# Moving gathered products past the additions into Y: a quota per operation instead of a common limit

## The chip, the core and the metric

The kernel runs on one core of one Trainium2 chip. The metric is device microseconds of one execution, from the first to the last instruction and what lies around them; the time of a kernel is the median of three runs. The engines are TensorE (PE in the rows; PEld is its weight load), VectorE (DVE), ScalarE (ACT), GpSimd (POOL), and SyncE (SP), which issues most transfers. Each engine works through its own instructions in the order in which they were written, and an instruction that waits holds up everything behind it on that engine.

## The reference, cut to what matters

One layer of an encoder: attention and retention, a normalization, and then a feed-forward layer with product keys (PEER), which is where the change lies. For each token `x` the layer picks 8 x 16 = 128 of 16,384 experts, with weights `g`:

```
act = gelu(einsum('tpkd,td->tpk', u_tab[eidx], x))
w   = g * act
out = einsum('tpk,tpkd->td', w, v_tab[eidx])
h   = layer_norm(ALPHA * h + out)
```

There are 1024 prompt tokens and 64 sample tokens, of 1024 channels each.

## The kernel before, in words

The tokens are cut into nine tiles of 128 rows: eight of the prompt and one, `TS`, of the sample. All run through the head first (projections, attention, retention, top-k), up to about 1290 us. Then comes the *dense stage*, the function `dense`, which does the experts in two ways at once.

- **Dense tiles** (five, `DENSE`): all 16,384 experts are computed on TensorE, 128 at a time. For each of the 128 blocks there is a *projection* `u_mm`: 48 matmuls into the PSUM tile `pA`, then a GELU on ScalarE, then on VectorE the product `ge` of it with the routing weights `gt`. Blocks go in groups of three (`BGS`). For each group come ten *value products* `v_mm`, one for each tile `t` and half `h` of the channels: nine matmuls into a PSUM tile `y`, of which there are two buffers (`pY`, `bufs=2`), and then on VectorE the addition of `y` into the SBUF tile `Y`. A third value product can only start when the addition of the first has read its buffer.
- **Gathered tiles** (four: `TS`, 5, 6 and 7): only the chosen experts are computed, on VectorE. A *slot* is one expert of each of the 128 tokens: GpSimd issues an indirect transfer (the *gather*, 128 rows of 8 KB, line 239) into one of four buffers `uv` (`NB = 4`); VectorE multiplies it with the tokens and sums (the *product*, out `uv`); ScalarE does the GELU and the weight (`gav`); VectorE adds the weighted row into `pacc` (the *accumulation*). There are 448 slots. The function `slot` writes one of these two instructions at each call, in turns: product of slot k, then accumulation of slot k-1. So a buffer is read for the last time by the accumulation that stands behind the next slot's product, and the gather four slots later waits for that.

The order on VectorE is decided while the program is written. `dense` is a generator that stops twice in each operation: after the matmuls are written, and after the work behind them is written (`ge`, or the addition into `Y`). At each stop the main loop calls `pump(most)`, which writes up to `2 * most` calls of `slot`, as long as a running estimate of the engines' times (`est`) says that VectorE is not ahead of TensorE and that the gather should have arrived. What is written at the first stop of a `v_mm` stands on VectorE ahead of its addition into `Y`. `prefetch` writes the next gathers, up to three slots ahead (`LEAD = 3`).

When the last slot of a gathered tile is accumulated, `finish` normalizes the tile. It goes on by one step (one `yield`) with each accumulation of the next tile: it loads the two rows of `ln2` into a tile `lnx`, which is one of the four gather buffers, takes statistics, and writes the two scaling instructions in `norm_out`. For `TS` it first moves half of the sum across partitions with a transfer and adds it.

All those instructions are recorded through one helper, so their line in the rows is L108; they are told apart by their tiles.

Of the kernel before, what the change touches and what calls it, by code (L numbers as in the profile page):

```python
# [52 lines left out]
ROOM = -0.3  # L53
# [82 lines left out]
def hymba_peer_step(ctx, tc, a, o):  # L136
# [16 lines left out]
    def rows_bcast(ap, n):  # L153
        return bass.AP(tensor=ap.tensor, offset=ap.offset, ap=[[0, 128], [1, n]])
# [51 lines left out]
    def halves(t):  # L206
        return [t[:, 0:512], t[:, 512:1024]]
# [4 lines left out]
    ctl = dict(most=3, k=0, issued=0, done=-1, avail=[0.0] * len(slots), fin=[], uvp=None, ln2=None, gps=None, lead=LEAD, slack=9.0, cr=0.0, pe0=0.0, dve0=0.0, ph=0, pq=0.0)  # L212
# [19 lines left out]
    def issue():  # L232
        k = ctl["issued"]
        t, j = slots[k]
        if t not in tl:
            open_tile(t)
        R = ctl["uvp"].tile([128, 2 * D], F32, name="uv", tag="uv")
        rows_uv[k] = R
        nc0.gpsimd.indirect_dma_start(out=R, out_offset=None, in_=a["uv"],  # L239
                                      in_offset=bass.IndirectOffsetOnAxis(ap=tl[t]["idx"][:, j:j + 1], axis=0))  # L240
        est.t["pool"] += 1.04
        ctl["pq"] = max(ctl["pq"], now()) + GTC
        est.t["dma"] = max(est.t["dma"], max(est.t["pe"], est.t["dve"]) - 3.0) + 2.6
        ctl["avail"][k] = max(est.t["dma"] + 2.0, max(ctl["pq"], now()) + ctl["slack"])
        ctl["issued"] = k + 1
# [25 lines left out]
    def finish(t, d):  # L271
        r, q = d["acc"], 128
        ln2, late = ctl["ln2"], t == TS
        if ln2 is None or t == TS:
            x = ctl["uvp"].tile([128, 2 * D], F32, name="lnx", tag="uv")
            ln2 = [x[:, 0:D], x[:, D:2 * D]]
            nc.sync.dma_start(ln2[0], rows_bcast(a["ln2_g"], D))
            if t == TS:
                q = NS
                nc.sync.dma_start(ln2[1][0:NS], r[NS:128])  # L280
                yield
                yield
                yield
                yield
                nc.vector.tensor_tensor(r[0:NS], r[0:NS], ln2[1][0:NS], op=OP.add)
            nc.sync.dma_start(ln2[1], rows_bcast(a["ln2_b"], D))
        yield from norm_out(gat, t, r, q, ln2)

    def norm_out(pool, t, r, q, ln2, st=None):
        wide = st is not None  # L290
        if not wide:
            st = pool.tile([128, 2, 6], F32, name="stf", bufs=2)
            for i, x in enumerate(halves(r)):
                nc.vector.bn_stats(st[:q, i], x[:q])
        mv = pool.tile([128, 3], F32, name="mvf", bufs=2)
        nc.vector.bn_aggr(mv[:q, 0:2], st[:q])
        nc.vector.tensor_scalar(mv[:q, 1:2], mv[:q, 1:2], EPS, None, op0=OP.add)
        nc.gpsimd.tensor_tensor(mv[:q, 2:3], mv[:q, 1:2], epsc[:q, 0:1], op=OP.pow)
        if wide:
            nc.gpsimd.tensor_tensor(mv[:q, 0:1], mv[:q, 0:1], mv[:q, 2:3], op=OP.mult)  # L300
            nc.gpsimd.tensor_scalar(mv[:q, 0:1], mv[:q, 0:1], -1.0, None, op0=OP.mult)
            yield
            nc.scalar.activation(r[:q], r[:q], AF.Identity, bias=mv[:q, 0:1], scale=mv[:q, 2:3])
            yield
            nc.gpsimd.tensor_tensor(r[:q], r[:q], ln2[0][:q], op=OP.mult)
            yield
            eng = nc.gpsimd if DENSE.index(t) in PAD else nc.vector
            eng.tensor_tensor(r[:q], r[:q], ln2[1][:q], op=OP.add)
            nc.sync.dma_start(o["y_p"][t * 128:(t + 1) * 128, :], r)
            return  # L310
        for _ in range(4):
            yield
        nc.vector.scalar_tensor_tensor(r[:q], r[:q], mv[:q, 0:1], ln2[0][:q], op0=OP.subtract, op1=OP.mult)
        yield
        nc.vector.scalar_tensor_tensor(r[:q], r[:q], mv[:q, 2:3], ln2[1][:q], op0=OP.mult, op1=OP.add)
        if t == TS:
            nc.sync.dma_start(o["y_s"], r[:q])
        else:
            nc.sync.dma_start(o["y_p"][t * 128:(t + 1) * 128, :], r)

    def can_slot():
        k = ctl["k"]
        return ctl["uvp"] is not None and k < len(slots) and ready[slots[k][0]]

    def prefetch():
        if ctl["uvp"] is None:
            return
        while (ctl["issued"] < len(slots) and ctl["issued"] < ctl["k"] + ctl["lead"]
               and ready[slots[ctl["issued"]][0]]):
            issue()  # L330
# [30 lines left out]
    def now():  # L361
        return max(est.t["pe"], est.t["dve"])
# [29 lines left out]
    def pump(most, room=1.0):  # L392
        prefetch()
        most = 2 * most
        while (can_slot() or ctl["ph"]) and most > 0:
            if est.t["dve"] > est.t["pe"] + room or (not ctl["ph"] and ctl["avail"][ctl["k"]] > now()):
                break
            slot()
            most -= 1
# [14 lines left out]
    bg, kind = [], []  # L414
# [823 lines left out]
    def dense(hx):  # L1238
# [205 lines left out]
        outs = []  # L1444
        for n, (kind, i) in enumerate(ops):
            last = kind == "v" and i[0] == NG - 1
            ctl["most"] = 4
            if n == SL[1]:
                ctl["slack"] = SL[2]
            if 2 <= n < 2 + NT:  # L1450
                nc.sync.dma_start(Y[:, n - 2], spill[DENSE[n - 2]]["h1"])
            if kind == "u":
                if i % 2 == 0:
                    g_load(i // 2 + 1)
                yield from u_mm(i)
            else:
                yield from v_mm(*i)
                if n == len(ops) - 2 * NT - 1:
                    ctl["ln2"] = [vp.tile([128, NT * 256], F32, name="ln2r", tag="gt", bufs=2)[:, 0:D] for _ in range(2)]
                    for x, k in zip(ctl["ln2"], ("ln2_g", "ln2_b")):  # L1460
                        nc.sync.dma_start(x, rows_bcast(a[k], D))
            if last:
                if can_slot():
                    slot()
                for g in outs:
                    next(g, None)
                if i[1]:
                    outs.append(norm_out(xp, DENSE[i[2]], Y[:, i[2]], 128, ctl["ln2"], yst[i[2]]))
            yield
# [14 lines left out]
    with ExitStack() as hx:  # L1484
        for _ in dense(hx):
            for _ in range(NBG):
                if ctl["uvp"] is not None and est.t["dve"] < est.t["pe"] + 1.0:
                    step_bg()
            pump(ctl["most"], ROOM)
        log("dense")  # L1490
        while bg:
            step_bg()
        drain()
# [112 lines left out]
```

## Time and profile before

| what | us |
|---|---|
| median of three runs (3319.77 to 3331.34) | 3320.02 |
| the profiled execution | 3355.53 |
| its span, first to last instruction | 3353.8 |

The profile is of one execution, which took 3355.53 us, some 35 us more than the median of the runs without a profile. Its span falls into the head (to about 1290 us), the part of the dense stage in which gathers run (1290 to 3130 us), the rest of the dense stage (to 3320 us) and an end of 34 us.

### The profile page before, as it was taken

The page shows a single profiled execution, that of the slowest core. Times are in us where ns is not written, and L with a number is a line of the kernel's source. Part 1 is how long each engine was busy: PE and PEld are TensorE (multiplying, and loading weights), DVE is VectorE, ACT ScalarE, POOL GpSimd, SP SyncE. Part 2 cuts the span into 40 slices and gives each one's busy share as a digit, 9 for nine tenths or more (in the row PEclk, how much of TensorE's full clock was granted, in tenths as well). Part 3 has the DMA queues.
Part 4 walks back from the last instruction along what each step waited for, and adds up shares of the span by engine and source line. Part 5 has one row for each costly group of instructions (what it writes and reads, how often), then busy time and mean ns, then how long its engine had stood idle before and what let it go on. Part 6 is the DMA issues. An engine that isn't in the chain of part 4 may idle for free.

```text
span 3353.8 us, 43782 instructions
## 1 busy us (share of the span) xinstructions
PE 2904.7 (87%) x15212; PEld 2495.5 (74%) x15212; DVE 2265.5 (68%) x5539; ACT 1115.8 (33%) x2599; POOL 1781.7 (53%) x1326
## 2 busy tenths in 40 slices
PE   4999889898996568888899988989899899989996
PEld 3777767677775557777788877878788788878895
DVE  1436976738639964776777777777778677877424
ACT  2332232332424663333333333333333333333221
POOL 0000155676663555665666666666666566666544
PEclk8999899899897789999999999999999999999998
DMA  6435235436432468898999989899989899999531
GB/s 178 145 112 213 82 84 145 95 62 167 97 79 79 114 181 325 326 346 304 349 355 354 350 336 340 321 347 341 355 323 361 318 349 349 351 367 340 199 98 63
DMA packets 296470, 813.19 MB, mean 242 GB/s; under 512 B 58296, under 2 KB 164520, under 8 KB 229176
## 3 DMA queue, kind: packets, MB, share of 16 engines
q0 software_dynamic: 97792, 469.94, 39.3%
q1 hardware_dynamic: 198024, 340.12, 29.9%
q8 instruction: 120, 1.97, 0.2%
q14 instruction: 102, 0.84, 0.1%
q10 hardware_dynamic: 432, 0.33, 0.0%
HBM read 753.04 MB, written 56.97 MB: 242 GB/s over the span
## 4 chain that ended last, share of the span: by engine, by line
PE 39%; DVE 22%; DMA 13%; issue 11%; POOL 10%; ACT 3%; SPq 1%; POOLq 0%; DVEq 0%; ACTq 0%
PE pA L108 13%; PE y L108 10%; DMA uv<-uv,gi 9%; PE pv L108 4%; PE pq L108 4%; DVE VI L108 4%; PE pa L108 3%; POOL uv L239 3%; POOL vl L108 3%; DVE pacc L108 3%; DVE ge L108 2%; DVE ob L108 2%; POOL ul L108 2%; POOL wl L108 2%; DVE oh L108 2%
## 5 line engine op out<-in xcount | busy, mean ns | idle before, releaser
L239 POOL DMA_INDIRECT uv<-uv,gi x448 | 432.1, 965 | 619.8 <-DVE pacc L108 561.2
L373 POOL DMA_INDIRECT G<-sg,si x256 | 382.3, 1493 | 620.2 <-DVE si L108 383.3
L108 DVE SCALAR_TENSOR_TENSOR uv<-uv,ph 128x1024 f32<-128x1024 f32 x448 | 544.1, 1215 | 238.1 <-DMA uv<-uv,gi 234.0
L108 PE MATMUL y<-vh,wh 128*128 128x512 f32 x1280 | 530.7, 415 | 185.1 <-DVE Y L108 182.9
L108 DVE SCALAR_TENSOR_TENSOR pacc<-uv,gav,pacc 128x1024 f32<-128x1024 f32 x448 | 575.6, 1285 | 2.2 <-ACT pacc L108 2.1
L108 PE MATMUL y<-vl,wh 128*128 128x512 f32 x1280 | 521.7, 408 | 2.0 <-POOL vl L108 2.0
L108 PE MATMUL y<-vh,wl 128*128 128x512 f32 x1280 | 520.8, 407 | 0.0
L108 PEld LDWEIGHTS y<-vh,wh 128*128 128x128 f32 x1280 | 250.8, 196 | 270.8 <-DVE Y L108 173.6
L108 DVE TENSOR_TENSOR Y<-y,Y 128x512 f32<-128x512 f32 x420 | 280.6, 685 | 178.8 <-PE y L108 175.1
L108 POOL TENSOR_TENSOR vl<-vr,vh 128x512 fp32r<-128x512 f32 x256 | 327.9, 1294 | 100.5 <-ACT vh L108 49.9
L108 PEld LDWEIGHTS pA<-xhi,uh 128*128 128x128 f32 x2048 | 331.5, 199 | 37.1 <-DVE ge L108 24.1
L108 PE MATMUL pA<-xhi,uh 128*128 128x320 f32 x2048 | 338.6, 320 | 23.3 <-DVE ge L108 23.3
L108 ACT ACTIVATE gav<-gav 128x1 f32<-128x1 f32 x448 | 88.7, 198 | 706.5 <-DVE uv L108 693.7
L108 PE MATMUL pA<-xlo,uh 128*128 128x320 f32 x2048 | 321.7, 309 | 0.0
L108 PE MATMUL pA<-xhi,ul 128*128 128x320 f32 x2048 | 321.2, 309 | 0.0
L108 POOL TENSOR_TENSOR ul<-ur,uh 128x1024 fp32r<-128x1024 f32 x128 | 309.6, 2418 | 4.8 <-ACT uh L108 2.5
L108 PEld LDWEIGHTS pA<-xlo,uh 128*128 128x128 f32 x2048 | 306.5, 188 | 0.0
L108 PEld LDWEIGHTS pA<-xhi,ul 128*128 128x128 f32 x2048 | 305.6, 187 | 0.0
L108 PEld LDWEIGHTS y<-vh,wl 128*128 128x128 f32 x1280 | 252.9, 198 | 57.0
L108 PEld LDWEIGHTS y<-vl,wh 128*128 128x128 f32 x1280 | 252.5, 197 | 48.9 <-POOL vl L108 2.9
L108 ACT ACTIVATE pA<-pA 128x640 f32<-128x640 f32 x128 | 88.0, 688 | 511.9 <-PE pA L108 505.9
L108 DVE TENSOR_TENSOR ge<-pA,gt 128x640 f32<-128x640 f32 x128 | 105.2, 822 | 212.0 <-ACT pA L108 145.3
(287 smaller groups left out, 4385.4 us busy)
## 6 DMA issues: line engine op xcount, KB each, us to landing
ur<-ut SPq DMA_DIRECT2D x128, 512.0 KB
vr<-vt SPq DMA_DIRECT2D x256, 256.0 KB
gt<-G SPq DMA_DIRECT2D x320, 128.0 KB
w<-w_r SPq DMA_DIRECT2D x32, 1024.0 KB
G<-gs SPq DMA_DIRECT2D x24, 1024.0 KB
G<-zeros SPq DMA_DIRECT2D x16, 1024.0 KB
w<-w_out SPq DMA_DIRECT2D x16, 1024.0 KB
w<-w_pq SPq DMA_DIRECT2D x16, 1024.0 KB
```

What stands on the lines that cost most here:

```text
L108: return f(*a, **k)
L239: nc0.gpsimd.indirect_dma_start(out=R, out_offset=None, in_=a["uv"], in_offset=bass.IndirectOffsetOnAxis(ap=tl[t]["idx"][:, j:j + 1], axis=0))
L373: nc0.gpsimd.indirect_dma_start(out=spill[t]["G"], out_offset=bass.IndirectOffsetOnAxis(ap=idx[:, j:j + 1], axis=0), in_=g[:, j:j + 1], in ...
```

## The change

The limit at each stop is replaced by a quota. At the first stop of a projection up to six calls of `slot` are written; at the first stop of a value product two calls if the tile's number `t` is odd, one call if it is even. At the second stop none is written; the main loop only calls `prefetch` there, and once more behind each `pump`. The two estimates that end `pump` early stay. In `finish` and `norm_out` steps are left out: the add for `TS` comes two accumulations earlier, and the first scaling instruction follows the statistics after one step instead of four. No instruction of the computation is added or removed.

```
@@ finish
                 yield
                 yield
-                yield
-                yield
                 nc.vector.tensor_tensor(r[0:NS], r[0:NS], ln2[1][0:NS], op=OP.add)
@@ norm_out
-        for _ in range(4):
-            yield
+        yield
         nc.vector.scalar_tensor_tensor(r[:q], r[:q], mv[:q, 0:1], ln2[0][:q], op0=OP.subtract, op1=OP.mult)
@@ dense
-            ctl["most"] = 4
+            ctl["most"] = 3 if kind == "u" else 1 if i[2] % 2 else 0.5
@@ the main loop
-            pump(ctl["most"], ROOM)
+            if ctl["most"]:
+                pump(ctl["most"], ROOM)
+                ctl["most"] = 0
+            prefetch()
```

What this does to the order is small. On TensorE the order is the same. The number of products in each group of three blocks stays at 9 to 13, and the last slot falls into the same group, the 38th of 43. On VectorE 126 of the 430 additions into `Y` come to stand ahead of an accumulation that stood ahead of them (122 of them of one accumulation, 4 of two), and 15 of the 128 `ge` likewise. About twenty products change sides as well.

The first place is on VectorE, in the group that runs at about 2227 to 2238 us before (`uv,gav` is a product, `pacc` an accumulation, `ge` the product behind a projection, `Y` an addition). Before:

```order
L108 SCALAR_TENSOR_TENSOR uv,gav<-uv,ph_16750 128x1024
L108 SCALAR_TENSOR_TENSOR pacc<-uv,gav,pacc 128x1024
L108 TENSOR_TENSOR ge<-pA,gt 128x640
L108 SCALAR_TENSOR_TENSOR uv,gav<-uv,ph_16750 128x1024
L108 SCALAR_TENSOR_TENSOR pacc<-uv,gav,pacc 128x1024
L108 TENSOR_TENSOR Y<-y,Y 128x512 x3
```

The same place in the changed kernel:

```order
L108 SCALAR_TENSOR_TENSOR uv,gav<-uv,ph_16750 128x1024
L108 SCALAR_TENSOR_TENSOR pacc<-uv,gav,pacc 128x1024
L108 TENSOR_TENSOR ge<-pA,gt 128x640
L108 SCALAR_TENSOR_TENSOR uv,gav<-uv,ph_16750 128x1024
L108 TENSOR_TENSOR Y<-y,Y 128x512
L108 SCALAR_TENSOR_TENSOR pacc<-uv,gav,pacc 128x1024
L108 TENSOR_TENSOR Y<-y,Y 128x512 x2
```

The first of the three additions has moved ahead of the second accumulation.

The second place is on VectorE too, at the end of the group before that (about 2185 to 2193 us). Before:

```order
L108 SCALAR_TENSOR_TENSOR pacc<-uv,gav,pacc 128x1024
L108 TENSOR_TENSOR Y<-y,Y 128x512 x2
L108 SCALAR_TENSOR_TENSOR uv,gav<-uv,ph_16750 128x1024
L108 SCALAR_TENSOR_TENSOR pacc<-uv,gav,pacc 128x1024
L108 TENSOR_TENSOR Y<-y,Y 128x512
```

The same place in the changed kernel:

```order
L108 TENSOR_TENSOR Y<-y,Y 128x512
L108 SCALAR_TENSOR_TENSOR pacc<-uv,gav,pacc 128x1024
L108 TENSOR_TENSOR Y<-y,Y 128x512
L108 SCALAR_TENSOR_TENSOR uv,gav<-uv,ph_16750 128x1024
L108 TENSOR_TENSOR Y<-y,Y 128x512
L108 SCALAR_TENSOR_TENSOR pacc<-uv,gav,pacc 128x1024
```

Both accumulations have moved behind an addition: the first behind the first of the pair, the second behind the addition that ends the group.

## Rows read from the trace of the kernel before

**Rows 1.** The page: the span, and busy time of each engine (part 1).

```profile
span 3353.8 us, 43782 instructions
PE 2904.7 (87%) x15212; PEld 2495.5 (74%) x15212; DVE 2265.5 (68%) x5539; ACT 1115.8 (33%) x2599; POOL 1781.7 (53%) x1326
```

**Rows 2.** Windows by stage: length, busy per engine (instructions), TensorE's clock, DMA share, GB/s.

```profile
1290.00:3130.00 1840.00, 1655.02 (x8779) 1471.51 (x8778) 1385.25 (x1840) 601.11 (x1463) 1158.05 (x897) 0.95 0.92 341
3130.00:3320.00 190.00, 187.90 (x1019) 168.76 (x1018) 60.81 (x89) 44.05 (x69) 84.41 (x57) 0.99 0.28 93
```

**Rows 3.** Waits, 1290 to 3130: engine, releaser, us in total, times, longest.

```profile
POOL uv L239 <- DVE pacc L108: 561.2, 266, 8.0
DVE uv L108 <- DMA uv<-uv,gi: 230.8, 111, 5.2
PE y L108 <- DVE Y L108: 180.8, 86, 8.7
...
DVE Y L108 <- PE y L108: 132.3, 82, 3.7
...
PE y L108 <- POOL vl L108: 2.0, 1, 2.0
```

**Rows 4.** Timeline of VectorE at the first place: start, length, [idle before, releaser].

```profile
2227.52 1.22 DVE L108 SCALAR_TENSOR_TENSOR uv<-uv,ph 128x1024 f32<-128x1024 f32 x1 [2.81 <-DMA uv<-uv,gi]
...
2228.67 1.29 DVE L108 SCALAR_TENSOR_TENSOR pacc<-uv,gav,pacc 128x1024 f32<-128x1024 f32 x1
2229.86 0.82 DVE L108 TENSOR_TENSOR ge<-pA,gt 128x640 f32<-128x640 f32 x1
2230.87 1.22 DVE L108 SCALAR_TENSOR_TENSOR uv<-uv,ph 128x1024 f32<-128x1024 f32 x1 [0.19 <-DMA uv<-uv,gi]
...
2232.01 1.28 DVE L108 SCALAR_TENSOR_TENSOR pacc<-uv,gav,pacc 128x1024 f32<-128x1024 f32 x1
2233.21 1.28 DVE L108 TENSOR_TENSOR Y<-y,Y 128x512 f32<-128x512 f32 x2
```

**Rows 5.** Timeline of TensorE at the first place.

```profile
2231.10 0.39 PE L108 MATMUL y<-vh,wl 128*128 128x512 f32 x1
2233.95 0.50 PE L108 MATMUL y<-vh,wh 128*128 128x512 f32 x1 [2.46 <-DVE Y L108]
```

**Rows 6.** Timeline of TensorE: the first and last of 31 stalls (text).

```profile
1345.06 0.79 PE L108 MATMUL y<-vh,wh 128*128 128x512 f32 x1 [8.68 <-DVE Y L108]
...
3111.03 0.50 PE L108 MATMUL y<-vh,wh 128*128 128x512 f32 x1 [3.23 <-DVE Y L108]
```

**Rows 7.** Windows: a stretch with a 0.53 us wait, one behind the 2.46 us wait.

```profile
2214.00:2221.00 7.00, 6.47 (x31) 5.17 (x30) 7.00 (x12) 2.99 (x9) 5.96 (x5) 1.00 0.85 291
...
2234.00:2238.00 4.00, 4.00 (x12) 3.23 (x13) 0.77 (x2) 0.00 (x0) 3.98 (x4) 0.57 0.99 395
```

**Rows 8.** Timeline of VectorE at the second place.

```profile
2187.80 1.29 DVE L108 SCALAR_TENSOR_TENSOR pacc<-uv,gav,pacc 128x1024 f32<-128x1024 f32 x1
2190.01 0.69 DVE L108 TENSOR_TENSOR Y<-y,Y 128x512 f32<-128x512 f32 x1 [0.93 <-PE y L108]
```

**Rows 9.** Timeline of VectorE: the first and last of 16 additions that waited (text).

```profile
1349.30 0.69 DVE L108 TENSOR_TENSOR Y<-y,Y 128x512 f32<-128x512 f32 x1 [3.70 <-PE y L108]
...
3080.12 0.69 DVE L108 TENSOR_TENSOR Y<-y,Y 128x512 f32<-128x512 f32 x1 [0.64 <-PE y L108]
```

**Rows 10.** Windows: the stretch with most transfers.

```profile
1622.00:1714.00 92.00, 87.57 (x490) 78.44 (x489) 75.96 (x101) 31.91 (x80) 61.85 (x48) 1.00 0.98 377
```

**Rows 11.** Timeline of GpSimd: the gather of the product at 2227.52 is issued.

```profile
2219.33 0.96 POOL L239 DMA_INDIRECT uv<-uv,gi  x1 [0.16 <-issue]
```

**Rows 12.** Timeline of SyncE and VectorE at the normalization of tile 5.

```profile
2092.45 0.33 SPq L85 DMA_DIRECT2D lnx<-ln_g  x1
...
2095.09 0.15 DVE L108 TENSOR_SCALAR mvf<-mvf 128x1 f32<-128x1 f32 x1
...
2116.64 1.28 DVE L108 SCALAR_TENSOR_TENSOR gacc<-gacc,mvf,lnx 128x1024 f32<-128x1024 f32 x1
```

## The prediction

> **What bounds the kernel now.** I read the page first: TensorE is busy 87% of the span, no other engine more than 74% [rows 1]. Then the windows by stage [rows 2]. The head has no changed instruction. From 3130 us on no gather is left, TensorE is busy 187.9 of 190 us and nothing can be gained. So what the change does, it does in the 1840 us from 1290 to 3130. There TensorE is busy 1655 us, VectorE 1385, and the transfer engines 0.92 of the time. Nothing is full, and TensorE, VectorE and the gathers wait for each other by turns. The table of waits says how [rows 3]: TensorE waits 181 us, in 86 places, for an addition into Y; VectorE waits 231 us, in 111 places, for a gather to land, and 132 us for the matmuls of an addition; GpSimd waits 561 us before gathers for the accumulation that frees the buffer, which alone costs nothing.
>
> The timeline of one place shows how the stalls come about [rows 4, 5]. A product waits 2.81 us for its gather. Behind it stand an accumulation, `ge`, another product, another accumulation, and only then two additions into Y. Their matmuls ended at about 2231.5, but the first addition starts at 2233.21, and TensorE, which has both `y` buffers full, stands still for 2.46 us. The gather in question had been issued at 2219.33 [rows 11], 8.2 us before its product could start.
>
> A stall costs a second time. In the 4 us behind this one the granted clock is 0.57, so mostly the lower level of 1.2 GHz; in a stretch of 7 us whose only wait on TensorE is 0.5 us it is 1.00 [rows 7]. The mean of the stage is 0.95 [rows 2]; going through the clock I count 35 stretches at half rate in it, 167 us in all, each behind a stall. Half of that, 84 us, is lost work.
>
> **The change part by part.** No engine gets more or less work, so all of it is a matter of waits.
>
> *Additions ahead of accumulations.* At the first place the change puts the first addition ahead of the second accumulation. It then starts when the product before it ends, at about 2232.0 and not 2233.2: the accumulation holds VectorE 1.2 us from its start to that of the next instruction [rows 4]. TensorE starts 1.2 us earlier too, since the next value product needs one buffer alone; the one behind it finds its buffer free at the same time as before, which is then early enough. I went through all 87 stalls of TensorE behind an addition (one lies at the border of the stage) and looked up in the order whether an accumulation leaves the front of that addition. It does in 31, which last 99.3 us together; the first and the last are [rows 6]. Taking 1.2 us from each, or all of it where it is shorter, gives **33 us**.
>
> *The clock behind them.* Of these 31 stalls 23 are followed by a stretch at half rate, 119 us in all, of which half is lost. I don't take all of it, since a stall that is shortened from 4 to 2.8 us may still be followed by one. Twelve of the 23 last 2.4 to 3.7 us and have 44 us at half rate behind them. They would last 1.2 to 2.5 us, and of the 24 stalls between 1 and 2.4 us that are in the trace now only 5 have a slow stretch behind them: about four fifths of 44/2, 18 us. Seven last 3.7 to 4.5 us and have 44 us behind them; they would be like the present ones of 2.5 to 3.3 us, which have one stretch of 3.4 us each, 24 us in all: (44-24)/2 = 10 us. The four longest I leave alone. Together **28 us**.
>
> *What the moved accumulations lose.* 126 accumulations now end later, by one addition of 0.69 us [rows 8] each: 87 us. Some lose more, because they used to run while the addition waited for its matmuls, as at 2187.80, where the addition then waits another 0.93 us [rows 8]. In 53 of the 126 places the matmuls had ended less than 1.28 us (one accumulation) before the addition started; in 16 of these VectorE waited outright [rows 9]. The shares of 1.28 us that no longer fit sum to 44 us. So buffers come free 131 us later in total, and the next gathers with them. Here I have to choose. If every gather had slack, nothing is lost; if none had, 131 us. The nearest row is the 111 products of 448 that wait for their gather now [rows 3], one in four: 33 us more of waits. And of what VectorE waits for gathers, 231 us, TensorE has 181 as stalls, so I take 0.78 of it: **26 us** lost, with 0 and 102 as bounds.
>
> *Accumulations moved behind `ge`.* 15 `ge` come 1.2 us earlier. `ge` frees `pA`, and the next projection comes only after three value products or more, so TensorE doesn't wait there; I take nothing. If a `ge` were what the stall behind it hangs on, it would be part of the stalls counted above, or at most 18 us more in gain.
>
> *Shorter normalization.* While `finish` runs, `lnx` holds one of four gather buffers. For tile 5 that is from 2092.45 to the scaling instructions that start at 2116.64 and about 5 us later [rows 12]. Three accumulations less, at some 4 us each (1840 us over 448 slots), give it back 12 us sooner; for `TS` five, 20 us. In windows of 46 us, the two with `TS` (1530 to 1622) have TensorE busy some 8 us less than two average ones, those of the other tiles some 2 us each. I give back two fifths: 5 us. Against it: the first scaling instruction needs `ln2_g`, issued at 2092.45, and would now come one product and one accumulation after 2095.24, at 2097.6 [rows 12]; if the load takes longer than 5 us VectorE waits, some 2 us in three places. Net **3 us**, between 5 and -6.
>
> *Prefetch at each stop.* The gathers stand at nearly the same places in GpSimd's order, ahead of the same splits of weights. They wait for the accumulation in any case, and TensorE waits for such a split only once in the stage, for 2 us [rows 3]. I take nothing, and a few us at most if a split comes to stand behind a later accumulation.
>
> **Sum.** 33 + 28 - 26 + 3 = 38 us off the profiled 3355.5 us, so 3317, 1.1%. The runs without a profile are 35 us shorter; scaled to their median, 3320 x (1 - 38/3355.5) = **3282 us**.
>
> **Rivals.**
>
> *The gathers take it back: no change.* Of the 61 us saved, all comes back if 61 us or so of the 131 us turn into stalls, somewhat less than half. For it speaks that VectorE waits for gathers longer than TensorE waits for VectorE [rows 3], and that a buffer goes round in only four slots. The transfers themselves could be the reason: at a share of 0.92 [rows 2] little is left. Against it: for 92 us, with the same mix of work, they ran at 377 GB/s and a share of 0.98, with TensorE at full clock and busy 95% [rows 10], while the stage's mean is 341. Taking 38 us out of the stage needs 341 x 1840/1802 = 348 GB/s. The time of this rival is 3320, within 0.5%. The Trainium skill ("DMA: Bandwidth & Descriptors", Specifications) gives about 358 GB/s as a core's limit at the HBM. By that the stage could lose no more than 1840 x (1 - 341/358) = 87 us; the trace, with 377 GB/s for 92 us, doesn't hold to that figure.
>
> *Accumulations held up by the matmuls: slower.* Place: an addition that waits for TensorE, as at 2190.01 [rows 8], now with an accumulation behind it that was ready. The gather four slots on is issued later by the whole wait, its product waits, and `ge` and the additions behind that product are late: the chain of [rows 4], made longer. Price: up to 131 us x 0.78 = 102 us as stalls, and a slower clock behind some of the new stalls. It decides against the change once more than about 80 of the 131 us become stalls (+17 us, 0.5%); at three quarters it is 98 - 64 = +34, a time of 3354. Against it: in the timeline gathers often queue behind each other, so a later issue doesn't always mean a later landing.
>
> *The stall goes with its cause: better than I say.* If the shortened stalls all lose their slow stretch (119/2 = 60 us in place of 28) and the lateness costs nothing, 33 + 60 + 5 = 98 us: 3223.
>
> **How the numbers follow.** My case, 3238 to 3303, has 0.63; the better one, below that, 0.03; no change 0.20; slower 0.14. The predicted time is 3282. A range of 3235 to 3338 leaves out the better case and most of the slower one, about 15 in 100; the forecast's own range is 3238 to 3303. Half a per cent, 16 us, is about what a measurement of this kernel can tell from no change (its three runs span 11.6 us). So faster 0.66, same 0.20, slower 0.14.
>
> **What would show it.** Right: from 1290 to the end of the gathers TensorE's waits for Y fall from 181 us to about 140, the stage's clock rises from 0.95 to 0.96 or 0.97, and the transfers' rate to about 348 GB/s; VectorE's waits for gathers stay near 231 or rise by up to 33. The stage is some 38 us shorter, and the 190 us behind it are as before. Wrong: waits for gathers rise by 60 us and more, while the waits for Y hold. What would make me wrong is the factor of one in four: if the gathers of the accumulations that were moved are mostly those that products wait for.

## The result, and the profile after

The changed kernel takes 3371.54 us (median; 3351.54 to 3375.54) beside 3327.23 us (3319.77 to 3333.15) of the kernel before, five runs each on one chip: a ratio of 1.0124 (95% interval 1.0100 to 1.0149). By the ratio it is 41 us slower (by the medians 44), where I forecast 38 us faster.

The page of the changed kernel answers to [rows 1], the windows by stage to [rows 2], the waits from 1290 to 3130 us to [rows 3]:

```profile
span 3349.7 us, 43800 instructions
...
PE 2890.7 (86%) x15212; PEld 2488.0 (74%) x15212; DVE 2268.3 (68%) x5539; ACT 1115.5 (33%) x2599; POOL 1781.0 (53%) x1326
```

```profile
1290.00:3130.00 1840.00, 1646.90 (x8760) 1467.30 (x8759) 1385.41 (x1837) 596.89 (x1457) 1152.09 (x894) 0.95 0.91 341
3130.00:3320.00 190.00, 182.76 (x978) 163.26 (x977) 59.21 (x91) 43.70 (x66) 84.49 (x59) 0.98 0.26 86
```

```profile
POOL uv L239 <- DVE pacc L108: 564.0, 237, 8.8
DVE uv L108 <- DMA uv<-uv,gi: 233.3, 133, 6.2
PE y L108 <- DVE Y L108: 181.8, 78, 11.8
...
DVE Y L108 <- PE y L108: 133.4, 108, 3.8
...
DVE gacc L108 <- DMA lnx<-gacc: 6.6, 1, 6.6
...
DVE gacc L108 <- DMA lnx<-ln_g: 3.9, 1, 3.9
```

Almost every total is that of before. TensorE's waits for Y did not fall from 181 us to 140; they stayed. VectorE's waits for gathers did not rise by 60 us either. Two waits are new: the add for `TS`, which comes two accumulations sooner, stands 6.6 us for its transfer, and a first scaling instruction 3.9 us for the rows of `ln2`.

These two profiles can't be set against each other, though: the execution of the kernel before that was profiled took 3355.5 us, longer than all its other runs, and that of the changed kernel was the fastest of its five. So the kernel before was profiled once more (e14 below; 3327.2 us, near its median). Its span is 3325.4 us; its window and waits:

```profile
1290.00:3130.00 1840.00, 1660.78 (x8894) 1477.75 (x8893) 1398.24 (x1856) 607.35 (x1476) 1170.41 (x905) 0.96 0.92 343
```

```profile
POOL uv L239 <- DVE pacc L108: 519.1, 254, 7.8
DVE uv L108 <- DMA uv<-uv,gi: 224.9, 126, 4.7
PE y L108 <- DVE Y L108: 177.2, 91, 8.4
DVE Y L108 <- PE y L108: 128.8, 91, 3.8
POOL wl L108 <- ACT wh L108: 44.0, 39, 7.3
```

In equal time its TensorE is busy 14 us longer (1660.78 against 1646.90) and runs 134 matmuls more, and its transfers move 343 GB/s, not 341. From the first addition into Y to the 380th, which ends the part with gathers, the second profile of before takes 1831.4 us and the changed kernel 1862.3, 31 us more. Going through the rows of TensorE there, I find 179.2 and 196.8 us of idle time, and 133 and 181 us at half rate, half of which is lost: 18 + 24 us. The remainder is 10.5 us smaller in the changed kernel; I have not traced that.

### The profile page after: what moved, and what is told of

Read it like the earlier page. It is cut to its first block, busy times and chain, and to the rows that moved or that the text cites. A ratio compares the mean times of both kernels' runs of the same rounds, so it can differ in the third digit from the quotient of the medians.

```text
span 3349.7 us, 43800 instructions
## 1 busy us (share of the span) xinstructions
PE 2890.7 (86%) x15212; PEld 2488.0 (74%) x15212; DVE 2268.3 (68%) x5539; ACT 1115.5 (33%) x2599; POOL 1781.0 (53%) x1326
## 4 chain that ended last, share of the span: by engine, by line
PE 33%; DVE 20%; issue 17%; POOL 16%; DMA 11%; ACT 2%; SPq 1%; POOLq 0%; DVEq 0%; ACTq 0%
PE pA L108 9%; PE y L108 8%; DMA uv<-uv,gi 7%; POOL uv L239 5%; POOL vl L108 5%; PE pq L108 4%; PE pv L108 4%; PE pa L108 3%; DVE VI L108 3%; POOL wl L108 3%; POOL ul L108 3%; DVE ge L108 2%; DVE ob L108 2%; DVE pacc L108 2%; DVE oh L108 2%
## 5 line engine op out<-in xcount | busy, mean ns | idle before, releaser
L108 POOL TENSOR_TENSOR vl<-vr,vh 128x512 fp32r<-128x512 f32 x256 | 327.7, 1293 | 98.9 <-ACT vh L108 46.6
```

Of the source, the lines that this page charges most:

```text
L108: return f(*a, **k)
```

## The experiments

The ratios are to the kernel before on the same chip, five rounds each. A ratio's interval is some 0.0024 on either side, so a difference of two is good to 0.0033, or 11 us; I give it as the difference of the ratios times 3330 us.

| run | kernel | ratio | interval |
|---|---|---|---|
| e1 | shorter normalization alone | 0.9937 | 0.9916 to 0.9959 |
| e2 | gathers ahead of splits alone | 1.0059 | 1.0038 to 1.0079 |
| e3 | additions ahead + shorter normalization | 1.0026 | 1.0006 to 1.0045 |
| e4 | gathers ahead + shorter normalization | 1.0026 | 1.0008 to 1.0043 |
| after | all three | 1.0124 | 1.0100 to 1.0149 |
| e5 | five buffers, shorter normalization | 0.9929 | 0.9904 to 0.9953 |
| e6 | five buffers, all three | 0.9887 | 0.9864 to 0.9909 |
| e7 | half gathers, shorter normalization | 0.9515 | 0.9494 to 0.9536 |
| e8 | half gathers, all three | 0.9518 | 0.9498 to 0.9538 |
| e9 | e5's smaller pools, four buffers | 1.0076 | 1.0055 to 1.0096 |
| e10 | e6's smaller pools, four buffers | 1.0214 | 1.0192 to 1.0236 |
| e11 | five buffers, as e3 | 0.9951 | 0.9933 to 0.9970 |
| e12 | five buffers, as e4 | 0.9884 | 0.9861 to 0.9907 |
| e13 | e1, and 32 additions ahead | 0.9937 | 0.9914 to 0.9960 |
| e14 | the kernel before again | 1.0003 | 0.9986 to 1.0021 |
| e15 | five buffers, as e13 | 0.9950 | 0.9931 to 0.9969 |
| e16 | five buffers alone | 0.9870 | 0.9845 to 0.9894 |
| e17 | five buffers, gathers ahead | 0.9853 | 0.9830 to 0.9875 |
| e18 | five buffers, additions and gathers ahead | 0.9821 | 0.9794 to 0.9848 |

### One part each (e1 to e4)

The change has three parts: additions that stand ahead of accumulations on VectorE, gathers written ahead of the splits of weights on GpSimd (the `prefetch` behind each `pump`), and the shorter normalization. A *split* is the subtraction on GpSimd that makes `ul`, `vl` or `wl`, the low part of an operand of the matmuls, once ScalarE has made its high part. Theory A blames VectorE's order, B GpSimd's, C the normalization. Edits of e1 and e2 against the kernel before, of e3 and e4 against the changed one:

```
e1 @@ finish and norm_out: the lines of the change, nothing else
e2 @@ the main loop
             pump(ctl["most"], ROOM)
+            prefetch()
e3 @@ the main loop
-            if ctl["most"]:
-                pump(ctl["most"], ROOM)
-                ctl["most"] = 0
-            prefetch()
+            pump(ctl["most"], ROOM)
+            ctl["most"] = 0
e4 @@ dense
-            ctl["most"] = 3 if kind == "u" else 1 if i[2] % 2 else 0.5
+            ctl["most"] = 3 if kind == "u" else 1
```

In e2 VectorE's order is word for word that of before, in e3 that of the changed kernel; in e4 the additions stand nearly where they stood before (19 of 430 moved, 7 of which move in e1 too). GpSimd's order, which the description of the change leaves out, differs as well: 71 of the 448 gathers in e2, and 70 in the changed kernel, stand ahead of a split, nearly always a `wl`, that stood ahead of them before.

> The kernel before with the shorter normalization steps alone; the order is otherwise that of before. Before is at 3327 us, the changed kernel at 3372. If the additions ahead of accumulations cause the loss (theory A): 3322 to 3332. If the gathers written behind each pump, which on GpSimd then stand ahead of a split of weights and make it wait for an accumulation, cause it (theory B): 3322 to 3332 too. If the shorter steps cause it, by waits for the rows of ln2 and the moved half of the sample tile (theory C): 3345 to 3370.

> The kernel before with one prefetch more behind each pump: VectorE's order is that of before to the instruction, and on GpSimd gathers move ahead of splits of weights as in the changed kernel. Theory A (VectorE's order): 3322 to 3332. Theory B (GpSimd's order): 3350 to 3370, with more waits of TensorE for weights that GpSimd or ScalarE split. Theory C (normalization): 3322 to 3332.

> The changed kernel with prefetch called only ahead of each pump, as before: VectorE's order is that of the changed kernel to the instruction, and GpSimd's is nearly that of before. Theory A: 3355 to 3375, as the changed kernel. Theory B: 3280 to 3330, since what the moved additions give would then show. Theory C: 3345 to 3370.

> The changed kernel with two calls ahead of every addition instead of one or two, so that no accumulation is parted from its product by an addition: VectorE's order is nearly that of before, GpSimd's that of the changed kernel, the normalization short. Theory A: 3322 to 3335. Theory B: 3350 to 3370. Theory C: 3345 to 3370.

Measured: the shorter normalization gains 21 us. On top of it the additions ahead cost 30 us (1.0026 against 0.9937), the gathers ahead 30 us, both together 62. The gathers ahead cost 20 us by themselves. The parts add up: -21 + 30 + 30 = 39, measured 41. So A and B both hold in part (e3 and e4 lie between what the two had expected of them), and C is the reverse.

What the gathers ahead do is seen on GpSimd, whose instructions run in order. The timeline of GpSimd at one place, in e14 (the order of before) and in e2:

```profile
1776.49 0.96 POOL L239 DMA_INDIRECT uv<-uv,gi  x1 [0.34 <-DVE pacc L108]
1780.63 1.57 POOL L108 TENSOR_TENSOR wl<-ge,wh 128x640 fp32r<-128x640 f32 x1 [3.17 <-ACT wh L108]
1782.39 0.96 POOL L239 DMA_INDIRECT uv<-uv,gi  x1 [0.19 <-issue]
```

```profile
1775.85 0.97 POOL L239 DMA_INDIRECT uv<-uv,gi  x1 [0.16 <-issue]
1781.89 0.95 POOL L239 DMA_INDIRECT uv<-uv,gi  x1 [5.07 <-PE y L108]
1782.84 1.58 POOL L108 TENSOR_TENSOR wl<-ge,wh 128x640 fp32r<-128x640 f32 x1
1784.37 1.30 POOL L108 TENSOR_TENSOR vl<-vr,vh 128x512 fp32r<-128x512 f32 x1
1785.83 0.96 POOL L239 DMA_INDIRECT uv<-uv,gi  x1 [0.16 <-DVE Y L108]
```

Before, the split `wl` runs while the next gather's buffer is still in use, and the gather goes out as soon as that is free. In e2 the gather stands first and waits 5.07 us. What it waits for is the accumulation on VectorE, which ends at 1781.61 (the row names TensorE, which had been done). Only then come the two splits, and the gather behind them starts 1.29 us after its own buffer came free at 1784.54. In the table of waits of e2 the idle time ahead of `wl`, 44.0 us in e14, is almost gone, and that in front of gathers has grown (the first row is 18.9 us in e14):

```profile
POOL uv L239 <- PE y L108: 58.8, 21, 5.1
...
POOL wl L108 <- ACT wh L108: 6.7, 6, 4.9
```

I measured this for every gather: from the end of the accumulation that frees its buffer (row of `pacc`, four slots back) to the start of the gather's row, which is 0.27 us at best. Of 444 gathers, 46 are over 1 us later than that in e14, 87 in e2, 33 in e1, 81 in e4, 93 in e3 and 140 in the changed kernel. (While `lnx` holds a buffer, a gather waits for the accumulation three slots back, not four; with that allowed for, some 30, 70, 30, 75, 85 and 130 are left, in the same order.) In e3 it is VectorE's order that does it: the accumulations come later, and the splits that used to run while a gather waited now run into it. In 89 of the 93 cases a split runs on GpSimd between the end of the accumulation and the gather, in 74 of them `ul` alone. From the start of a product to the end of its accumulation the mean is 6.94 us in e14, 6.93 in e1, 7.18 in e3 and 7.24 in the changed kernel.

### A fifth gather buffer, and half gathers (e5 to e8)

Theory D: both costs are paid through the ring of four buffers. A (VectorE's order is worse whatever the gathers do) and B (splits come late for TensorE) are its rivals, and E: the transfers themselves set the pace. A fifth buffer needs room, which is taken from other pools; gathers are still written three slots ahead, so no order changes:

```
-NB, LEAD = 4, 3
+NB, LEAD = 5, 3
...
-        idx = gat.tile([128, 128], I32, name="gi", bufs=2)
+        idx = gat.tile([128, 128], I32, name="gi", bufs=1)
...
-                v = vp.tile([128, 512], F32, name="vr", bufs=5)
+                v = vp.tile([128, 512], F32, name="vr", bufs=3)
...
-            ge = up.tile([128, ND], F32, name="ge")
+            ge = up.tile([128, ND], F32, name="ge", bufs=1)
```

The half gathers (e7, e8):

```
-        nc0.gpsimd.indirect_dma_start(out=R, out_offset=None, in_=a["uv"],
+        nc0.gpsimd.indirect_dma_start(out=R[:, 0:D], out_offset=None, in_=a["uv"].rearrange("e (h d) -> (e h) d", h=2),
...
-        nc.vector.scalar_tensor_tensor(acc, rows_uv[k][:, D:2 * D], d["av"][:, j:j + 1], acc,
+        nc.vector.scalar_tensor_tensor(acc, rows_uv[k][:, 0:D], d["av"][:, j:j + 1], acc,
```

> The kernel with the shorter normalization alone, and a fifth gather buffer: gathers are still written three slots ahead, so every engine's order is word for word that of the kernel with the shorter normalization alone (3314 us), but a gather waits for the accumulation one slot earlier. Room for it comes from three raw buffers vr instead of five, one ge instead of two and one table of indices instead of two. Theory D, the ring of four gather buffers sets the pace of the stage and the stalls of TensorE are what the ring leaves over: GpSimd's wait before gathers (564 us) falls by far more than half, VectorE's waits for gathers fall by 60 us or more, and the time falls to 3250 to 3280. Rival E, the transfers themselves set the pace (they are busy nine tenths of the stage), so an earlier issue only queues longer: 3305 to 3325, with VectorE's waits for gathers near 200 us. The smaller pools may cost some us under both.

> The changed kernel with the same fifth gather buffer and the same smaller pools, its order unchanged. Under theory D the late accumulations and the gathers written ahead of the splits no longer lengthen a ring, and the additions that stand further ahead still start earlier: the 57 us that the changed kernel stands behind the one with the shorter normalization alone shrink to 15 or less, or turn into a gain. Rival A (VectorE's order itself is worse, whatever the gathers do) and rival B (the splits of weights come late behind waiting gathers) keep 25 us or more each of the 57 between this kernel and the one with five buffers and the shorter normalization alone; under B TensorE's waits for a split, one of 2 us before, would add up to 20 us or more.

> The kernel with the shorter normalization alone, whose gathers fetch half: rows of 4 KB instead of 8 KB, from a table that is read as rows of half the length, and both the product and the accumulation read that half, so the computed values are others; every instruction stands where it stood. It takes half of the gathers' bytes away and leaves four buffers. Theories D and E both expect VectorE's waits for gathers to fall below 100 us and the time to 3230 to 3270, because a gather lands sooner. If the waits for gathers fall and the time stays within 15 us of 3314, the gathers never set the pace.

> The changed kernel whose gathers fetch half in the same way (other values are computed, the order is the changed kernel's). If the price of the changed order is paid through gathers that come late (theory D or E), it is gone here, and what I forecast for the additions that stand further ahead shows: this kernel is 0 to 40 us below the one with the shorter normalization alone and half gathers. If VectorE's order itself is worse (rival A), or the splits behind waiting gathers (rival B, since GpSimd still waits for the buffers), it stays 25 us or more above it.

The sign turns. With four buffers the changed kernel is 62 us behind the shorter normalization alone; with five it is 14 us ahead (0.9887 against 0.9929), with half gathers it is level (0.9518 and 0.9515). So neither order is worse by itself, and A and B, as they are put here, fall: the price is paid through gathers that come late. That the fifth buffer hardly moved e5 itself (0.9929 after 0.9937) looked like rival E by its time, but its waits are those of D: GpSimd's wait before gathers fell from 514.8 us in e1 to 62.0, VectorE's waits for gathers from 203.5 to 134.8. The control below shows what took the time back. The rows of e5:

```profile
DVE uv L108 <- DMA uv<-uv,gi: 134.8, 100, 7.6
...
POOL uv L239 <- DVE pacc L108: 62.0, 46, 10.0
```

That the transfers matter too is plain from e7: it moves 224 GB/s where the kernel with full gathers moves 344, and is 141 us faster, more than either theory had expected. Its window and one of its waits:

```profile
1290.00:3130.00 1840.00, 1770.85 (x9760) 1589.36 (x9759) 1430.07 (x1908) 641.68 (x1531) 1241.92 (x949) 0.99 0.69 224
```

```profile
DVE uv L108 <- DMA uv<-uv,gi: 56.9, 49, 2.8
```

### Controls, and single parts with five buffers (e9 to e12)

e9 and e10 are e5 and e6 with `NB = 4`; e11 and e12 are e3 and e4 with the edit of the fifth buffer.

> The control of the five buffers: the shorter normalization alone, the smaller pools (three vr, one ge, one table of indices), but four gather buffers as before. What the smaller pools cost shows against the kernel with the shorter normalization alone, at 0.995 of the kernel before. If the fifth buffer is what moved the time, this kernel lies at 1.000 to 1.010 of the kernel before (the smaller pools cost 15 to 50 us, which the fifth buffer more than made good); if the smaller pools themselves were the gain, it lies near the 0.993 of the five buffers.

> The changed kernel with the smaller pools and four gather buffers. Theory D, the changed order pays through the ring of gather buffers: it stays 40 us or more behind the same pools with the shorter normalization alone, so at 1.015 to 1.025 of the kernel before, while with five buffers it was 14 us ahead. Rival: the smaller pools shift the work of ScalarE and SyncE so that the changed order no longer costs anything; then the two lie within 15 us, and the fifth buffer has nothing to do with it.

> Five gather buffers, the additions ahead of accumulations as in the changed kernel, the shorter normalization, but gathers not written ahead of the splits. With four buffers this cost 26 us on top of the shorter normalization. Under theory D it costs nothing here, and gains what was forecast for the additions in part: 3280 to 3305, against 3305 for the shorter normalization alone. If VectorE's order itself is worse, 3325 or more.

> Five gather buffers, the gathers written ahead of the splits as in the changed kernel and the shorter normalization, but the additions into Y nearly where they stood before. With four buffers this cost 27 us on top of the shorter normalization. If it costs because a gather that waits for its buffer holds up the splits behind it on GpSimd, the wait is gone with the fifth buffer: 3290 to 3310. If an earlier issue itself hurts (gathers queue in front of the loads of weights), it still costs 15 us or more: 3320 to 3335.

The smaller pools cost 46 us with the shorter normalization and 30 with the changed kernel; the fifth buffer then gives back 49 and 109. With the smaller pools and four buffers the changed order costs 46 us, with five it gains 14. So it is the buffer, as D says. By parts, with five buffers: the gathers ahead gain 15 us (21 where the additions stand ahead too: e6 against e11); the additions ahead cost 7 without them and 1 with them, which is nothing that can be measured. e11 does not show the gain that I had expected in part.

### Where the shortened stalls went (e13 to e16)

For each value product I took the idle time of TensorE ahead of its first matmul, and sorted the products by whether the addition that frees its buffer had left an accumulation behind. From e14 to the changed kernel the stalls at those products fall from 98.7 to 52.3 us, and all others rise from 78.5 to 139.5. With five buffers (e5 to e11) they go from 73 to 34 and from 86 to 142, with half gathers (e7 to e8) from 37 to 13 and from 29 to 56. By place: the third value product behind a group's first projection has 98.9 us of stalls in e14 and 55.7 in the changed kernel, the third behind the second projection 35.5 and 70.3, the third behind the last 34.8 and 65.8. Theory P says that displaced accumulations now stand in front of those other additions, rival R that what TensorE saves at one place it waits for at the next. e13 moves only the first addition of each group, ahead of one accumulation:

```
+            ctl["q"] = kind == "v" and i[1] * NT + i[2] < 1
-            ctl["most"] = 4
+            ctl["most"] = 4 if not ctl["q"] else 1 if i[2] % 2 else 0.5
@@ the main loop
             pump(ctl["most"], ROOM)
+            if ctl["q"]:
+                ctl["most"] = 0
```

e15 adds the fifth buffer to e13, e16 to the kernel before.

> The shorter normalization, and of the changed order only this: the first value product of each group gets a quota of one call, so 32 first additions come to stand ahead of one accumulation, which then stands between the first and the second addition; no other addition moves, and GpSimd's order stays. These 32 gate the stalls of the third value product behind a group's first projection, 90 to 100 us in the kernel with the shorter normalization alone. Theory P, the time came back because displaced accumulations were put in front of other additions: that happens nowhere here, except at the second addition, which has time, so the stalls fall by 25 to 38 us, no others rise, and the time is 15 to 35 us below the shorter normalization alone (0.983 to 0.989 of the kernel before). Rival R, TensorE's stalls are what the loop through the gathers leaves over: those stalls fall just as much, others behind the next two projections rise as much, and the time stays within 8 us (0.991 to 0.996).

> The kernel before, unchanged: a second profile of it, and a ratio of 0.998 to 1.002. Under theory D more than a gather late at GpSimd is the mark of the changed order, so the gathers that are issued over 1 us behind the accumulation that frees their buffer should be about 48 of 444 again, as in its first profile.

> The same 32 additions with five gather buffers and the smaller pools. Under theory P it gains 15 to 35 us on five buffers with the shorter normalization alone (which is at 0.993), so 0.982 to 0.989; under R, where the loop is looser now, 5 to 20 us (0.987 to 0.9915).

> The kernel before, longer normalization and all, with five gather buffers and the smaller pools. If the shorter normalization gains its 16 us because the rows of ln2 take one of four gather buffers away for a shorter while, a fifth buffer leaves four and the gain shrinks to 0 to 6 us: 0.993 to 0.995 of the kernel before. If it gains by work that no longer stands in front of additions on VectorE, it keeps 12 us or more: 0.9965 or above.

e14 strays by 0.0003 from the kernel that it is, and has 46 late gathers where the first profile of before has 48. e13 gains nothing on e1 (0.9937 both), and e15 nothing on e5 (0.9950 against 0.9929), where R had expected some gain too. In e13 the stalls behind the 32 moved additions fall from 87.3 to 41.5 us, more than I had forecast for them, and the others rise from 79.2 to 119.5, though no other addition moved. P falls and R holds. One group shows how. VectorE's and TensorE's timeline in e1 (of TensorE the first matmul of the first value product, of the third, of the third behind the second projection, and of the first behind the last projection):

```profile
2256.69 1.22 DVE L108 SCALAR_TENSOR_TENSOR uv<-uv,ph 128x1024 f32<-128x1024 f32 x1 [4.14 <-DMA uv<-uv,gi]
...
2260.90 1.28 DVE L108 SCALAR_TENSOR_TENSOR pacc<-uv,gav,pacc 128x1024 f32<-128x1024 f32 x1
2262.10 1.28 DVE L108 TENSOR_TENSOR Y<-y,Y 128x512 f32<-128x512 f32 x2
...
2270.79 1.22 DVE L108 SCALAR_TENSOR_TENSOR uv<-uv,ph 128x1024 f32<-128x1024 f32 x1 [0.68 <-DMA uv<-uv,gi]
...
2278.88 1.28 DVE L108 TENSOR_TENSOR Y<-y,Y 128x512 f32<-128x512 f32 x2
```

```profile
2255.06 0.39 PE L108 MATMUL y<-vh,wh 128*128 128x512 f32 x1
...
2262.83 0.79 PE L108 MATMUL y<-vh,wh 128*128 128x512 f32 x1 [3.51 <-DVE Y L108]
...
2279.71 0.47 PE L108 MATMUL y<-vh,wh 128*128 128x512 f32 x1 [0.61 <-DVE Y L108]
...
2288.91 0.40 PE L108 MATMUL y<-vh,wh 128*128 128x512 f32 x1
```

The same group in e13:

```profile
2249.37 1.22 DVE L108 SCALAR_TENSOR_TENSOR uv<-uv,ph 128x1024 f32<-128x1024 f32 x1 [2.87 <-DMA uv<-uv,gi]
...
2253.58 0.68 DVE L108 TENSOR_TENSOR Y<-y,Y 128x512 f32<-128x512 f32 x1
2254.19 1.28 DVE L108 SCALAR_TENSOR_TENSOR pacc<-uv,gav,pacc 128x1024 f32<-128x1024 f32 x1
...
2264.12 1.22 DVE L108 SCALAR_TENSOR_TENSOR uv<-uv,ph 128x1024 f32<-128x1024 f32 x1 [2.79 <-DMA uv<-uv,gi]
...
2268.48 1.22 DVE L108 SCALAR_TENSOR_TENSOR uv<-uv,ph 128x1024 f32<-128x1024 f32 x1 [1.21 <-DMA uv<-uv,gi]
...
2270.82 1.28 DVE L108 TENSOR_TENSOR Y<-y,Y 128x512 f32<-128x512 f32 x2
```

```profile
2249.46 0.39 PE L108 MATMUL y<-vh,wh 128*128 128x512 f32 x1
...
2254.32 0.50 PE L108 MATMUL y<-vh,wh 128*128 128x512 f32 x1 [0.59 <-DVE Y L108]
...
2271.65 0.77 PE L108 MATMUL y<-vh,wh 128*128 128x512 f32 x1 [3.85 <-DVE Y L108]
...
2283.68 0.39 PE L108 MATMUL y<-vh,wh 128*128 128x512 f32 x1
```

The addition has moved ahead of the accumulation, the first stall falls from 3.51 to 0.59 us, and TensorE comes to the second projection early. VectorE does not: its next products wait 2.79 and 1.21 us for gathers, and the additions behind them are late, so TensorE waits 3.85 us there and runs at half rate behind that. From the group's first value product to the last mark it is 33.85 us in e1 and 34.22 in e13. Over the stage VectorE's waits for TensorE fall by 14 us and its waits for gathers rise by 26; these rows answer to each other, e1 first:

```profile
DVE uv L108 <- DMA uv<-uv,gi: 203.5, 114, 5.3
...
DVE Y L108 <- PE y L108: 131.8, 84, 3.7
```

```profile
DVE uv L108 <- DMA uv<-uv,gi: 229.5, 128, 4.8
...
DVE Y L108 <- PE y L108: 117.9, 90, 3.8
```

e16 came out as neither expectation had it: with five buffers the longer normalization is 20 us faster than the shorter one (0.9870 against 0.9929). In e5 VectorE stands still for the rows that `finish` loads and for the half of `TS` that it moves, 14.4 us in the two rows below, and e16 has no such row; what the rest of the 20 us is, I have not traced:

```profile
DVE gacc L108 <- DMA lnx<-ln_g: 10.3, 1, 10.3
...
DVE gacc L108 <- DMA lnx<-gacc: 4.1, 1, 4.1
```

### The version that the experiments point to (e17, e18)

Five buffers, the longer normalization, and the gathers ahead (e17) or the whole changed order (e18).

> Five gather buffers and the smaller pools, the longer normalization of the kernel before, its order on VectorE, and the gathers written ahead of the splits. If the two gains of five buffers add (15 us for the gathers ahead, 17 us for not waiting for the rows of ln2), it is the fastest of all: 3265 to 3282, 0.980 to 0.985 of the kernel before. If they are the same gain (VectorE standing still until a gather lands), 0.986 to 0.989, as with either alone.

> The whole changed order (additions ahead of accumulations, gathers ahead of splits) with five gather buffers and the longer normalization. Against the changed kernel with five buffers (0.9887) it shows the shorter normalization: 10 to 20 us less (0.983 to 0.986) if the shorter one costs because VectorE waits for the rows of ln2, the same if that was an accident of one order. Against the run beside it, it shows the additions ahead of accumulations: within 8 us if what they save comes back at the next stalls.

e18 is the fastest of the kernels with full gathers, 0.9821, 3274.58 us beside 3333.64 of the kernel before. With five buffers, taking the shorter normalization out of the changed kernel gains 22 us (0.9821 against 0.9887). The gains of e17 add only in part. Between e17 and e18 lie 11 us, the width of the uncertainty and a little over the 8 that I had expected at most: the additions ahead gain little or nothing here too. e18's window and waits, to be read beside those of e14:

```profile
1290.00:3130.00 1840.00, 1698.33 (x9224) 1517.51 (x9223) 1411.29 (x1874) 618.33 (x1498) 1196.70 (x921) 0.98 0.90 347
```

```profile
PE y L108 <- DVE Y L108: 136.7, 80, 5.7
POOL uv L239 <- DVE pacc L108: 128.7, 81, 4.3
...
DVE uv L108 <- DMA uv<-uv,gi: 96.2, 87, 5.4
```

Its waits for Y and its rate are near what I had forecast of the changed kernel (140 us, 348 GB/s), bought with a buffer.

## Why the prediction was wrong

*Additions ahead of accumulations, 33 us, and the clock behind them, 28 us.* The stalls that I counted shrank as forecast or better: by 46 us from e14 to the changed kernel, by 46 in e13. The step that failed is the sentence that the next value product finds its buffer "at the same time as before, which is then early enough", taken as the end of the matter. A stall that goes at one place lets TensorE reach the next one sooner, but VectorE's next additions stand behind products that wait for gathers, and those did not come sooner. So the stall came back one or two projections on, with its slow stretch: TensorE spends 150 us at half rate in e1's stage and 147 in e13's. With nothing else moved (e13, e15), or with gathers light (e8, where the gathers ahead are in it too), the net is zero within 11 us. In my terms 61 us of gain measured 0; what 32 later accumulations lose, 7 us by my prices, is within that zero.

*What the moved accumulations lose, 26 us.* The lateness came out near: 131 us forecast; from the start of a product to the end of its accumulation, measured, 0.25 us more for each of 448 slots in e3 than in e1, 112 us, and 0.3 us, 134 us, more in the changed kernel than in e14. The price came near too, if the gain is taken as the zero of e13: the additions ahead cost 30 us in all (e3). But the factor of one in four has no run of its own, and the forecast lacks a way in which part of that is paid: the lateness pushed gathers behind splits that had run in their waiting time, 93 late gathers instead of 33. How much goes which way is not shown, so that 26 is close to 30 is luck. The whole kernel came near the +34 us of the rival of the accumulations held up, and that is no confirmation either: the place that I had named there, an addition that waits for TensorE, hardly changed (128.8 us in e14, 133.4 in the changed kernel), and the sum of the parts has GpSimd's queue in it, which the rival doesn't.

*Prefetch at each stop, nothing.* This failed outright: 20 to 30 us. That the gathers stand at nearly the same places in GpSimd's order, ahead of the same splits, was misread: 70 of 448 stand ahead of one more. And I argued that gathers wait for the accumulation in any case. They do, but what stands behind a waiting gather on GpSimd waits with it: the splits, and behind them the next gather. That I said TensorE hardly ever waits for a split was true and beside the point; the price is paid by the next gather. With the fifth buffer, where GpSimd waits far less for accumulations (128.7 us before gathers in e18, 519.1 in e14), the same edit gains 6 to 21 us (e17 on e16, e12 on e5, e6 on e11), the 6 being within the noise.

*Shorter normalization, 3 us.* Right in sign, too small: 21 us, beyond my bound of 5. I had seen one cost, a wait for the rows of `ln2`; the changed kernel has 3.9 us of it, and 6.6 us for the transfer of `TS`, which I had not priced. With five buffers, where there is little to give back, a cost remains (20 us). That the gain comes from the buffer that `lnx` gives back sooner fits this turn of sign, but the smaller pools were there too, so it is argued and not shown.

*`ge`, nothing,* was not tested by itself.

The forecast's sum was -38; by the measured parts it is -21 + 30 + 30 = +39. The sign that I had named for being wrong, waits for gathers 60 us longer, did not show: they are 224.9 us in e14 and 233.3 in the changed kernel. Of the rivals, "the gathers take it back" describes the additions of e13; "held up" has the kernel's time, by another way. The Trainium skill's figure of about 358 GB/s ("DMA: Bandwidth & Descriptors", Specifications) was no limit here either: the page of e18 shows slices of 82 us, a fortieth of its span, at up to 388 GB/s (the row below). The Trainium skill ("HBM Reference", Specifications (TRN2)) has it too that a core streaming alone measures well above its share, and with that the trace agrees.

```profile
GB/s 173 156 117 206 90 93 130 91 88 156 90 94 49 123 162 233 384 370 345 346 388 368 337 369 330 339 342 374 336 344 364 357 355 372 372 366 369 197 98 68
```

## What to carry to other kernels

Where two engines and a ring of transfers wait for each other by turns, the sum of an engine's stalls is no measure of what an edit at those stalls gives: ask whether the work in front of the next stall also comes sooner; if that hangs on a transfer, the gain can come back as a stall there, as it did here. When an instruction that waits is moved ahead of one that could have run in its waiting time, price what stands behind both on the same queue, down to the next transfer. And settle first what the loop lacks: with one more buffer, two of the three parts of this change turned from a loss of 30 us each to a gain or nothing, and the third from a gain of 21 us to a loss of 20.

## What the runs showed of the hardware that I had not expected

The same program with nearly the same stalls can lose very different time to the clock. In the two profiles of the kernel before, TensorE idles 187 and 179 us in the stage and does the same work, but 171 us and 133 us of it are granted at 1.2 GHz instead of 2.4, behind 36 and 32 stalls; that is 19 of the 24 us by which the two stages differ (1855.4 and 1831.4 us). A profile of one execution can thus lie further from its median than the change that is looked for. And the three raw buffers `vr`, with one `ge` and one table of indices, cost 30 to 46 us (e9, e10), as much as each part of the change.
